# Modulation by raw float32 matmuls in pieces, with the mixer's branches and conv taps in another order

## The chip, the cores and the metric

The program runs on one core of one Trainium2 chip. The metric is the device time of one execution in microseconds; lower is better. The kernel before takes 2353.6 us (median of three runs, 2352.47 to 2354.03).

## The reference

Two blocks follow each other. The change is in the first alone: two layers of a token mixer and a gated FFN on 256 tokens `x` and, in layer 0, 256 context tokens `ctx`, with a modulation vector in front.

```python
for l in range(DEPTH):                                   # DEPTH = 2, D_MODEL = 1024
    mod  = silu(c) @ w_mod[l] + b_mod[l]                 # [1024] @ [1024, 6144]
    modc = silu(c_ctx) @ w_mod[l] + b_mod[l]
    sh1, sc1, gt1, sh2, sc2, gt2 = split(mod, 6)         # and the same of modc for ctx
    h = rms_norm(xl, g_pre_mix[l]) * (1 + sc1) + sh1
    y, yc = token_mixer(h, hc, ...)                      # conv branch, diff attention, pool branch, gates, w_out
    xl = xl + gt1 * rms_norm(y, g_post_mix[l])
    h = rms_norm(xl, g_pre_ffn[l]) * (1 + sc2) + sh2
    xl = xl + gt2 * rms_norm(swiglu(h, w_ffn_in[l], w_ffn_out[l]), g_post_ffn[l])
# token_mixer: g = sigmoid(h @ w_g + b_gate)
# m = g[0:1024] * y_a + g[1024:2048] * y_b + g[2048:3072] * y_c;  return m @ w_out
```

`y_a` is a depthwise convolution of 31 taps with layer norm, `y_b` differential attention of 8 heads, `y_c` a multi-scale pool. All arithmetic is float32. The modulation of a layer reads a weight of 1024 x 6144 and multiplies it by two vectors, `c` and `c_ctx`.

## The kernel before

Activations lie transposed, features on the 128 partitions and tokens in the columns: 512 columns in layer 0 (both streams), 256 in layer 1. A weight of 1 MB (1024 x 256) is loaded by SP into one of two raw buffers, then split into a high part (ACT, L154) and a low part (DVE or POOL, L155) of the float32r type. Each product is three matmuls (`mm3`, L164 to L166). A ring of four split pieces per kind lets `emit` prepare weights ahead of the step that uses them.

The program is a list of steps with costs. `merge` spreads a side list over a main list by cost, and `emit` walks the list. Below it a scheduler sets the order on each engine, and each engine then works through its own queue in that order: what stands in front and waits holds up what is behind.

The modulation of layer 0's first sections (columns 0 to 2047, four groups of 512) is computed in the set-up by `mod` (L433): 32 loads of 128 x 512, each split by L257 and L258, and 64 matmuls of 512 columns (L447, L448) whose stationary side holds the high and low parts of the two vectors in four of 128 columns; `mod_flush` (L498) then copies and transposes the result. The other 20 groups of 512 columns are computed by `mod_v` (L462) on DVE: L476 and L478 multiply 128 x 512 tiles by a scalar per partition and add them up, and a flush (L484) sums over the partitions with matmuls of a 128 x 128 float32 weight tile against one column of ones; L489 adds the bias. Six of these groups run beside the mixer's last branches in layer 0, the rest beside layer 0's FFN. Their loads are 512 KB each in a ring of two (`mraw`).

`mixer1` (L747) orders the mixer of a layer: the gated linear unit of the convolution; then `qkv(0)` with 20 conv taps; four head pairs of attention, each merged with the next pair's q, k, v (the fourth with `gates(0)`) and a quarter of the 104 taps left; then the attention's closing norm `o_fin`, the pool linear with the convolution's layer norm, `w_conv_out` with the pool windows, `gates(2)`, the pool's group products, `w_pool_out`, and at last the gates of the attention and `w_attn_out` in turn. Half of the taps run on DVE (L795), half on ACT and POOL (L792, L793). Scores are half-array matmuls (L742), transposes stand at L869. Between the mixer and FFN0 stands a join: sums over features (L611, L612), the residual and the norm for the second half of the tokens (L316).

Of the kernel before, what the change touches and what calls it, by code (L numbers as in the profile page):

```python
# [26 lines left out]
SHARE = (2, 2, 0, 0, 4, 0, 0, 0)  # of 8 weight pieces, how many GpSimd subtracts, by phase  # L27
SLOTS, RING, MORE, RAWS, US, MRAWS = 66, 4, 4, 2, 6, 2
# [7 lines left out]
class Two:  # L36
    """[128, 8, n] in two tiles"""
# [8 lines left out]
class Kern:  # L46
# [64 lines left out]
    def pieces(self, loads, na, nb, cuts, perm=False):  # L111
        box = {}
        out = []
        for i, (a0, a1, b0, b1) in enumerate(cuts):
# [86 lines left out]
    def lin_pair(self, st, Wa, ca, Wb, cb, n, rhs, N, evac_a, evac_b):  # L201
        """tiles of two column ranges in turn, two by two"""
# [32 lines left out]
    def lin_nat(self, st, W, c0, lhs, ntok, evac):  # L235
        """out [128 tokens, 256 columns]; lhs(t) -> [(hi, lo)] per k tile, [128, 128 tokens]"""
# [50 lines left out]
    def sq_add(self, key, src, N, i, n):  # L287
        """adds src^2 to the running sum self.v[key]"""
# [12 lines left out]
    def col_rms(self, key, nt, dim):  # L301
        """sums over features (partitions) and then 1/rms per token: [128 tokens, nt]"""
# [9 lines left out]
    def bcast(self, r, nt, ps=None, at=0):  # L312
        """[128 tokens, nt] -> PSUM [128, 128 nt]: the same row of tokens on each partition"""
# [29 lines left out]
    def setup(self):  # L343
# [24 lines left out]
        self.st1 = self.const([128, 8, 128], "st1", F32R)  # L368
        nc.vector.memset(self.st1.bitcast(F32), 0.0)
        v = cc.rearrange("p (s k) -> p k s", s=2)  # L370
        nc.vector.tensor_copy(self.st1[:, :, 0:2], v)
        nc.vector.tensor_tensor(self.st1[:, :, 2:4], v, self.st1[:, :, 0:2], op=ALU.subtract)
        self.cc = cc
        self.mc = [self.const([128, 48, 2], f"mc{l}") for l in range(2)]
        nc.gpsimd.memset(self.mc[1], 0.0)
# [57 lines left out]
    def mod(self, l, g):  # L433
        """512 columns on the tensor engine: rows c, c_ctx of the high parts, then of the low parts"""
# [7 lines left out]
        def f():  # L442
            ps = self.lin_ps()
            for k in range(8):
                hi, lo = self.slot(F32R), self.slot(F32R)
                self.split(hi, lo, raw[k])
                nc.tensor.matmul(ps, self.st1[:, k], hi, start=k == 0, stop=False)  # L447
                nc.tensor.matmul(ps, self.st1[:, k], lo, start=False, stop=k == 7)  # L448
            self.mod_flush(l, g, ps)
        return f  # L450

    def pin(self, inst):
        """keeps an instruction that waits for nothing from taking its tile far ahead of its turn"""
        self.tc.keep_in_program_order(inst)

    def mraw(self, l, g, h):
        w = self.wp.tile([128, 2, 512], F32, name=self.nm("mraw"), tag="mraw", bufs=MRAWS)
        self.nc.sync.dma_start(w, self.a["w_mod"][l, 256 * h:256 * h + 256, 512 * g:512 * g + 512].rearrange(
            "(k p) c -> p k c", p=128))
        return w  # L460

    def mod_v(self, st, l, groups, streams):  # L462
        """the same with the products and their sums over k tiles on the vector engine"""
        nc = self.nc
        accs = {}

        def part(g, h):
            w = self.mraw(l, g, h)
            if h == 0:
                accs[g] = [self.slot() for _ in range(streams)]  # L470
            for k in range(2):
                for i in range(streams):
                    acc = accs[g][i]
                    c = self.cc[:, 8 * i + 2 * h + k:8 * i + 2 * h + k + 1]
                    if h == 0 and k == 0:
                        nc.vector.tensor_scalar(acc, w[:, k], c, None, op0=ALU.mult)  # L476
                    else:
                        nc.vector.scalar_tensor_tensor(acc, w[:, k], c, acc, op0=ALU.mult, op1=ALU.add)  # L478

        def flush(g):  # L480
            ps = self.tr_ps()
            for i in range(streams):
                for t in range(4):
                    nc.tensor.matmul(ps[:, 4 * i + t:4 * i + t + 1], accs[g][i][:, 128 * t:128 * t + 128],  # L484
# [1440 lines left out]
```

## Time and profile before

| what | value |
|---|---|
| median of three runs | 2353.6 us (2352.47 to 2354.03) |
| span of the profiled execution, its own time | 2355.8 us |
| PE busy | 2197.7 us, 93% |
| DVE busy | 1707.7 us, 72% |
| ACT busy | 1095.3 us, 46% |
| POOL busy | 536.5 us, 23% |
| matmul records | 14576 |

The span is the time from the first to the last recorded instruction of one profiled execution; the record gives no other time for that execution, so the sums of the prediction stand on 2355.8. PE means the matmuls of TensorE and PEld its weight loads, which overlap them; DVE is VectorE, ACT ScalarE, POOL GpSimd, SP the engine that issues the loads. PEclk in a window is the TensorE clock that was granted, as a share of full speed. The durations of single matmuls overlap, so a cost per matmul is read from the distance between them: a window's length divided by its count.

### The profile page before, as it was taken

The numbers are of one execution on the slowest core, as the hardware profiler recorded it, in microseconds if no ns is written. First come the engines' busy times: TensorE is split into PE (matmuls) and PEld (weight loads), VectorE is DVE, ScalarE is ACT, GpSimd is POOL, SyncE is SP. The second block draws the span as 40 slices with busy tenths as digits, with TensorE's granted clock in tenths as the row PEclk, the third lists the DMA queues.
The fourth block names the chain that finished last, engine by engine and source line by source line (L and its number), as shares of the span: only waits on it lengthen the run. The fifth ranks groups of instructions, "written<-read, shape, count | busy, mean of one in ns | idle before, by whom it ended". The sixth has DMA issues, their size and how long they took to land.

```text
span 2355.8 us, 37801 instructions
## 1 busy us (share of the span) xinstructions
PE 2197.7 (93%) x14576; PEld 1998.8 (85%) x14576; DVE 1707.7 (72%) x3443; ACT 1095.3 (46%) x2110; POOL 536.5 (23%) x545
## 2 busy tenths in 40 slices
PE   4978889999989999989999899999889999999998
PEld 3767777788888888878788899999877999988998
DVE  5697987959678745578988877764686766686665
ACT  5436565332332222244566554554446544465543
POOL 2344433321340110143333312100342000210000
PEclk8989999999999999998999999999987999999999
DMA  7312112335414555553322454455541555542553
GB/s 271 93 55 67 54 59 72 123 132 170 152 63 154 168 179 170 170 165 108 108 72 90 148 174 160 154 193 176 160 90 37 176 183 177 177 144 84 185 180 125
DMA packets 296628, 319.21 MB, mean 135 GB/s; under 512 B 20544, under 2 KB 264352, under 8 KB 296448
## 3 DMA queue, kind: packets, MB, share of 16 engines
q1 hardware_dynamic: 293072, 311.27, 41.1%
q0 software_dynamic: 2224, 3.43, 0.6%
q8 instruction: 114, 1.87, 0.3%
q10 hardware_dynamic: 1152, 2.10, 0.3%
q14 instruction: 66, 0.54, 0.1%
HBM read 315.72 MB, written 1.05 MB: 134 GB/s over the span
## 4 chain that ended last, share of the span: by engine, by line
PE 66%; DVE 21%; issue 4%; ACT 3%; DMA 3%; POOL 1%; SPq 0%; ACTq 0%; DVEq 0%; POOLq 0%
PE p L164 19%; PE p L165 19%; PE p L166 19%; DVE wlo L155 3%; DVE t L795 3%; DVE t L478 2%; DVE t L258 2%; PE p L742 1%; DVE b L851 1%; DMA mraw<-in_w_mod_dram 1%; DVE t L725 1%; PE tr L484 1%; DMA raw<-in_w_in_dram 1%; PE p L247 1%; ACT whi L154 1%
## 5 line engine op out<-in xcount | busy, mean ns | idle before, releaser
L164 PE MATMUL p<-t,whi 128*128 128x256 f32 (+1 forms) x3724 | 1175.5, 320 | 20.8 <-ACT t L560 8.5
L165 PE MATMUL p<-t,whi 128*128 128x256 f32 (+1 forms) x3724 | 1183.0, 319 | 5.6 <-DVE t L561 2.1
L166 PE MATMUL p<-t,wlo 128*128 128x256 f32 (+1 forms) x3724 | 1178.2, 318 | 6.4 <-DVE wlo L155 4.8
L164 PEld LDWEIGHTS p<-t,whi 128*128 128x128 f32 x3724 | 718.8, 195 | 72.6 <-ACT t L560 10.3
L165 PEld LDWEIGHTS p<-t,whi 128*128 128x128 f32 x3724 | 723.6, 194 | 50.8 <-DVE t L659 3.5
L166 PEld LDWEIGHTS p<-t,wlo 128*128 128x128 f32 x3724 | 723.1, 194 | 50.4 <-DVE wlo L155 5.9
L154 ACT ACTIVATE whi<-raw 128x1024 fp32r<-128x1024 f32 (+4 forms) x487 | 492.0, 1020 | 543.4 <-PE p L165 332.6
L155 DVE TENSOR_TENSOR wlo<-raw,whi 128x1024 fp32r<-128x1024 f32 (+4 forms) x443 | 545.4, 1232 | 201.7 <-ACT whi L154 113.7
L155 POOL TENSOR_TENSOR wlo<-raw,whi 128x1024 fp32r<-128x1024 f32 (+2 forms) x44 | 103.5, 2353 | 503.6 <-ACT whi L154 464.8
L478 DVE SCALAR_TENSOR_TENSOR t<-mraw,big,t 128x512 f32<-128x512 f32 x224 | 176.6, 827 | 17.7 <-DMA mraw<-in_w_mod_dram 16.2
L793 POOL TENSOR_TENSOR t<-t,t 128x512 f32<-128x512 f32 (+1 forms) x120 | 134.9, 1125 | 186.0 <-ACT t L792 178.5
L594 POOL TENSOR_TENSOR t<-t,t 128x256 f32<-128x256 f32 (+1 forms) x68 | 70.4, 1063 | 246.1 <-ACT t L596 242.8
L299 POOL TENSOR_TENSOR t<-t,t 128x256 f32<-128x256 f32 (+1 forms) x27 | 25.6, 948 | 430.6 <-ACT t L297 430.1
L260 ACT ACTIVATE t<-t 128x256 fp32r<-128x256 f32 (+1 forms) x115 | 54.3, 473 | 148.9 <-DVE t L689 104.4
L742 PE MATMUL p<-t,t 64*128 64x256 f32 (+2 forms) x528 | 78.5, 374 | 28.5 <-DVE t L261 9.8
L247 PE MATMUL p<-whi,t 128*128 128x256 f32 x352 | 101.8, 289 | 2.8 <-ACT t L853 1.6
L248 PE MATMUL p<-wlo,t 128*128 128x256 f32 x352 | 99.8, 284 | 0.0
L249 PE MATMUL p<-whi,t 128*128 128x256 f32 x352 | 99.8, 283 | 0.0
L689 DVE TENSOR_TENSOR t<-t,p 128x256 f32<-128x256 f32 (+1 forms) x91 | 43.1, 474 | 76.8 <-PE p L166 76.6
L795 DVE SCALAR_TENSOR_TENSOR t<-u,big,t 128x512 f32<-128x512 f32 (+1 forms) x120 | 94.9, 791 | 1.5
L742 PEld LDWEIGHTS p<-t,t 64*128 64x128 f32 x528 | 50.9, 206 | 49.2 <-issue 16.8
L257 ACT ACTIVATE t<-t 128x256 fp32r<-128x256 f32 (+1 forms) x92 | 43.2, 495 | 100.0 <-DVE t L725 80.6
(299 smaller groups left out, 2717.0 us busy)
## 6 DMA issues: line engine op xcount, KB each, us to landing
raw<-in_w_in_dram SPq DMA_DIRECT2D x60, 1024.0 KB, 5.1
raw<-in_l_w_gate_up_dram SPq DMA_DIRECT2D x44, 1024.0 KB, 5.1
raw<-in_w_ffn_in_dram SPq DMA_DIRECT2D x42, 1024.0 KB, 5.3
mraw<-in_w_mod_dram SPq DMA_DIRECT2D x80, 512.0 KB, 4.0
raw<-in_l_w_in_dram SPq DMA_DIRECT2D x15, 1024.0 KB, 5.2
raw<-in_l_w_down_dram SPq DMA_DIRECT2D x16, 896.0 KB, 4.9
t<-in_w_mod_dram SPq DMA_DIRECT2D x32, 256.0 KB, 5.4
raw<-in_w_attn_out_dram SPq DMA_DIRECT2D x8, 1024.0 KB, 5.2
```

Source lines behind the costliest of these rows:

```text
L154: nc.scalar.activation(p.hi, src, AF.Copy)
L155: eng.tensor_tensor(p.lo, src, p.hi, op=ALU.subtract)
L164: mm(ps, lh, rh, start=first, stop=False)
L165: mm(ps, lh, rl, start=False, stop=False)
L166: mm(ps, ll, rh, start=False, stop=last)
L247: mm(ps[:, :256], lh, p.hi[:, k % 4], start=k == 0, stop=False)
L248: mm(ps[:, :256], lh, p.lo[:, k % 4], start=False, stop=False)
L249: mm(ps[:, :256], ll, p.hi[:, k % 4], start=False, stop=k == 7)
L478: nc.vector.scalar_tensor_tensor(acc, w[:, k], c, acc, op0=ALU.mult, op1=ALU.add)
L742: self.nc.tensor.matmul(out[half], q[i // 2][h, qs], k[i % 2][h, ks], start=i == 0, stop=i == 2)
L793: nc.gpsimd.tensor_tensor(acc, acc, t, op=ALU.add)
L795: nc.vector.scalar_tensor_tensor(acc, u, w, acc, op0=ALU.mult, op1=ALU.add)
```

## The change

All of the modulation becomes matmuls with a raw float32 tile of `w_mod` (128 x 128) as the stationary side and the two vectors as two moving columns, summed over eight k tiles in PSUM; one DVE add of the bias ends it. In the set-up the four groups keep their loads, and 128 such products (`mod_mm`, L432 of the changed kernel) take the place of the splits and of the 64 matmuls of 512 columns. The other 80 output tiles become units (`mods`): a 512 KB load into a ring of two, eight products, one add. Forty go among the attention steps of layer 0 (ten per head pair), eight (layer 1's section 0) behind the join in front of FFN0, 32 among the attention steps of layer 1 (10, 10, 10, 2). `mod_v` is gone.

The branches are in another order: `gates(2)` instead of `gates(0)` beside the fourth pair; then the pool branch with `w_pool_out`, which now starts the merged sum; then the rest of `gates(0)`, the convolution's layer norm and `w_conv_out`; the attention's part comes last as before. The 124 taps are spread over a longer stretch: 17 beside `qkv(0)` and each of three pairs, 23 beside the fourth, 33 beside the pool branch.

```diff
-SLOTS, RING, MORE, RAWS, US, MRAWS = 66, 4, 4, 2, 6, 2
+SLOTS, RING, MORE, RAWS, US, MODS = 64, 4, 4, 2, 7, 2
...
+    def mod_mm(self, ps, w, k):
+        c = self.cc.rearrange("p (s k) -> p k s", s=2)[:, k]
+        self.nc.tensor.matmul(ps, w, c, start=k == 0, stop=k == 7)
+    def mod_out(self, l, j, n, ps):
+        b = self.par["b_mod", l][:, j:j + n]
+        self.nc.vector.tensor_tensor(self.mc[l][:, j:j + n, :], ps.rearrange("p (t s) -> p t s", s=2),
+                                     b[:, :, None].to_broadcast([128, n, 2]), op=ALU.add)
...
+            if last:
+                ps = [self.lin_ps()[:, :2] for _ in range(4)]
+                for k in range(8):
+                    for t in range(4):
+                        self.mod_mm(ps[t], raw[k][:, 128 * t:128 * t + 128], k)
...
             ps = self.lin_ps()
-            for k in range(8):
-                hi, lo = self.slot(F32R), self.slot(F32R)
-                self.split(hi, lo, raw[k])
-                nc.tensor.matmul(ps, self.st1[:, k], hi, start=k == 0, stop=False)
-                nc.tensor.matmul(ps, self.st1[:, k], lo, start=False, stop=k == 7)
-            self.mod_flush(l, g, ps)
+            for t in range(4):
+                for k in range(8):
+                    self.mod_mm(ps[:, 2 * t:2 * t + 2], raw[k][:, 128 * t:128 * t + 128], k)
+            self.mod_out(l, 4 * g, 4, ps[:, :8])
...
+        def unit(j):
+            p = Piece()
+            p.ring = 2
+            def prep():
+                p.hi = self.static("mraw", 1024, MODS).rearrange("p (a b) -> p a b", a=8)
+                nc.sync.dma_start(p.hi, self.a["w_mod"][l, :, 128 * j:128 * j + 128].rearrange(
+                    "(k p) c -> p k c", p=128))
+            def f():
+                ps = self.lin_ps()[:, :2]
+                for k in range(8):
+                    self.mod_mm(ps, p.hi[:, k], k)
+                self.mod_out(l, j, 1, ps)
+            p.prep = prep
+            return ("x", 0.9, f, (p,))
+        return [unit(8 * s_ + i) for s_ in secs for i in range(8)]
...
-        out += merge(qkv(0), conv[:20])
-        ncv = len(conv) - 20
+        taps = iter(conv)
+        take = lambda n: [t for _, t in zip(range(n), taps)]
+        out += merge(qkv(0), take(17))
+        fill = iter(fill)
         for pr in range(4):
-            main = qkv(pr + 1) if pr < 3 else gates(0)
-            side = att(pr)
-            out += merge(merge(main, side), conv[20 + pr * ncv // 4: 20 + (pr + 1) * ncv // 4])
-        out.append(X(o_fin))
+            main = qkv(pr + 1) if pr < 3 else gates(2)
+            side = merge(att(pr), [t for _, t in zip(range(10), fill)])
+            out += merge(merge(main, side), take(17 if pr < 3 else 23))
         pl = []
         self.lin(pl, W, 4096, 512, hx, N, pool_evac)
+        out += merge(pl, take(11) + [X(o_fin)])
...
+        g0 = gates(0)
+        out += merge(merge(g0[:4], rest), take(11))
+        gr = groups()
+        b3 = []
+        self.lin(b3, a["w_pool_out"][l], 0, 1024, lambda: V["z"], N, merge_c, K=4)
+        out += gr + merge(b3, list(taps))
         side = [X(conv_ln), X(conv_ln2)] + [X(lambda m=m: conv_ln3(m)) for m in range(4)]
-        out += merge(pl, side)
+        out += merge(g0[4:], side, 1)
...
-            fs = [self.mod(0, g) for g in (2, 3, 0, 1)]
+            fs = [self.mod(0, g, g == 1) for g in (2, 3, 0, 1)]
...
+            fill = self.mods(0, (2, 4, 3, 5)) + self.mods(1, (1,)) if l == 0 else self.mods(1, (2, 4, 3, 5))
...
             st += jm(256 if l == 0 else 0, True)
+            if l == 0:
+                st += self.mods(1, (0,))
...
-                self.mod_v(ms, 0, (10, 11), 2)
...
-                self.mod_v(ms, 1, (2, 3, 0, 1), 2)
-                self.mod_v(ms, 1, (4, 5, 8, 9, 6, 7, 10, 11), 1)
```

How the change stands in the queues is shown at three places on PE. A name such as `p_1315` is a PSUM tile, the buffers behind the arrow are the stationary and the moving side, and a closing `x8` is a row repeated.

In the attention of layer 0, before, the scores (L742) of a head pair follow each other and the next linear tile comes behind them:

```order
L742 MATMUL p_1336<-t_1065,t_970 128x512
L742 MATMUL p_1337<-t_1065,t_970 128x512
L742 MATMUL p_1364<-t_1065,t_969 128x256
L742 MATMUL p_1364<-t_1066,t_969 128x256
L742 MATMUL p_1364<-t_1065,t_970 128x256
L742 MATMUL p_1365<-t_1065,t_969 128x256
L742 MATMUL p_1365<-t_1066,t_969 128x256
L742 MATMUL p_1365<-t_1065,t_970 128x256
L164 MATMUL p_1387<-t_505,whi_1134 128x512
L165 MATMUL p_1387<-t_506,whi_1134 128x512
L166 MATMUL p_1387<-t_505,wlo_1135 128x512
L164 MATMUL p_1387<-t_507,whi_1134 128x512
```

After, units of eight products (L432) stand among the scores (now L722), here two of them in front of the next linear tile:

```order
L722 MATMUL p_1205<-t_969,t_875 128x512
L722 MATMUL p_1206<-t_969,t_875 128x512
L432 MATMUL p_1224<-big,mraw 128x2 x8
L722 MATMUL p_1237<-t_969,t_874 128x512
L722 MATMUL p_1238<-t_969,t_874 128x512
L722 MATMUL p_1237<-t_970,t_874 128x512
L722 MATMUL p_1238<-t_970,t_874 128x512
L722 MATMUL p_1237<-t_969,t_875 128x512
L722 MATMUL p_1238<-t_969,t_875 128x512
L432 MATMUL p_1256<-big,mraw 128x2 x8
L722 MATMUL p_1275<-t_969,t_874 128x256
L722 MATMUL p_1275<-t_970,t_874 128x256
```

So each unit is a block of eight products between pieces of the attention on the same queue.

At the join before FFN0, before, the sums over features (L611, L612) alternate with matmuls of FFN0 for the tokens of the first half (the tile `p_6372`, with `whi_5965` of its weight):

```order
L164 MATMUL p_6372<-t_5899,whi_5965 128x256
L165 MATMUL p_6372<-t_5900,whi_5965 128x256
L166 MATMUL p_6372<-t_5899,wlo_5966 128x256
L164 MATMUL p_6372<-t_5901,whi_5965 128x256
L612 MATMUL tr_6152<-big,t_6142 128x1
L611 MATMUL tr_6152<-big,t_5518 128x1
L612 MATMUL tr_6152<-big,t_6142 128x1
L611 MATMUL tr_6152<-big,t_5520 128x1
L612 MATMUL tr_6152<-big,t_6144 128x1
L611 MATMUL tr_6152<-big,t_5520 128x1
L612 MATMUL tr_6152<-big,t_6144 128x1
L611 MATMUL tr_6152<-big,t_5522 128x1
```

After, units stand between the norm's transposes (L318), and the tile `p_6481` of FFN0 comes behind all eight:

```order
L432 MATMUL p_6376<-big,mraw 128x2 x8
L318 MATMUL tr_6267<-big,c_6251 128x128 x2
L432 MATMUL p_6387<-big,mraw 128x2 x8
L432 MATMUL p_6398<-big,mraw 128x2 x8
L318 MATMUL tr_6267<-big,c_6281 128x128 x2
L432 MATMUL p_6461<-big,mraw 128x2 x8
L432 MATMUL p_6471<-big,mraw 128x2 x8
L166 MATMUL p_6481<-t_6014,whi_6410 128x256
L167 MATMUL p_6481<-t_6015,whi_6410 128x256
L168 MATMUL p_6481<-t_6014,wlo_6411 128x256
L166 MATMUL p_6481<-t_6016,whi_6410 128x256
```

The matmuls of FFN0 that filled the join before are now behind the units, whose loads come through a ring of two buffers.

In the set-up, before, a group's sixteen matmuls of 512 columns (`st` holds the vectors) stand together and the transposes of `x` (L1104) behind them:

```order
L447 MATMUL p_181<-t_218,st_97 128x512
L448 MATMUL p_181<-t_219,st_97 128x512
L447 MATMUL p_181<-t_224,st_97 128x512
L448 MATMUL p_181<-t_225,st_97 128x512
L1104 MATMUL p_273<-big,t_74 128x128
L1104 MATMUL p_273<-big,t_78 128x128
L1104 MATMUL p_273<-big,t_82 128x128
L1104 MATMUL p_273<-big,t_86 128x128
```

After, the first products against two columns lie between those transposes (now L1085):

```order
L432 MATMUL p_176<-big,t_112 128x2
L1085 MATMUL p_244<-big,t_74 128x128
L1085 MATMUL p_244<-big,t_78 128x128
L1085 MATMUL p_244<-big,t_82 128x128
L432 MATMUL p_176<-big,t_114 128x2
L1085 MATMUL p_244<-big,t_86 128x128
L1085 MATMUL p_251<-big,t_74 128x128
L1085 MATMUL p_251<-big,t_78 128x128
L1085 MATMUL p_251<-big,t_82 128x128
L432 MATMUL p_176<-big,t_116 128x2
L1085 MATMUL p_251<-big,t_86 128x128
```

The stationary side is now the loaded tile itself, with no split in front of it.

## Rows read from the trace of the kernel before

**Rows 1.** The page: span, busy time by engine, engines of the last chain

```profile
span 2355.8 us, 37801 instructions
...
PE 2197.7 (93%) x14576; PEld 1998.8 (85%) x14576; DVE 1707.7 (72%) x3443; ACT 1095.3 (46%) x2110; POOL 536.5 (23%) x545
...
PE 66%; DVE 21%; issue 4%; ACT 3%; DMA 3%; POOL 1%; SPq 0%; ACTq 0%; DVEq 0%; POOLq 0%
```

**Rows 2.** Windows of four stages: us, busy us (count) of five engines, PEclk, DMA share

```profile
120.00:160.00 40.00, 28.66 (x176) 24.99 (x174) 39.61 (x53) 13.76 (x24) 17.24 (x13) 0.88 0.24 79
160.00:336.00 176.00, 154.82 (x936) 129.86 (x937) 152.10 (x324) 104.76 (x261) 74.98 (x54) 0.96 0.16 51
336.00:390.00 54.00, 53.20 (x283) 42.60 (x281) 32.61 (x68) 33.82 (x79) 19.57 (x13) 1.00 0.21 70
1157.60:1281.10 123.50, 114.28 (x772) 101.18 (x771) 109.21 (x234) 73.26 (x172) 39.80 (x50) 0.97 0.25 81
```

**Rows 3.** Waits of PE in 160 to 336: us in total, times, longest

```profile
PE p L742 <- DVE t L261: 9.8, 2, 7.0
PE tr L869 <- DVE t L861: 9.3, 9, 1.8
```

**Rows 4.** PE groups by form in 160 to 336: count, busy us, mean ns, idle before

```profile
L164 PE MATMUL p<-t,whi 128*128 128x512 f32 x97 | 41.0, 422 | 2.3 <-DVE t L261 2.3
...
L742 PE MATMUL p<-t,t 64*128 64x256 f32 x69 | 8.6, 316 | 9.8 <-DVE t L261 9.8
```

**Rows 5.** Windows of two flushes and of two dense stretches

```profile
482.94:484.64 1.70, 1.70 (x17) 1.70 (x16) 0.00 (x0) 1.65 (x2) 0.54 (x1) 1.00 1.00 346
1058.88:1061.44 2.56, 2.56 (x13) 2.56 (x14) 0.00 (x0) 0.00 (x0) 0.00 (x0) 0.50 0.00 0
930.00:950.00 20.00, 20.00 (x89) 16.53 (x89) 12.62 (x17) 4.74 (x7) 2.50 (x1) 1.00 0.59 188
1900.00:1950.00 50.00, 50.00 (x419) 50.00 (x418) 33.22 (x53) 24.59 (x36) 0.00 (x0) 1.00 0.57 188
```

**Rows 6.** DVE groups by form: one tap, one add of the modulation

```profile
L795 DVE SCALAR_TENSOR_TENSOR t<-u,big,t 128x512 f32<-128x512 f32 x60 | 60.2, 1003 | 0.7
...
L489 DVE TENSOR_TENSOR big<-tr,big 128x4 f32<-128x4 f32 x32 | 4.3, 156 | 33.5 <-PE tr L484 33.2
```

**Rows 7.** DMA issues: count, KB each, median us to landing

```profile
raw<-in_w_ffn_in_dram SPq DMA_DIRECT2D x4, 512.0 KB, 4.0
```

**Rows 8.** Windows of three neighbouring stretches around 682.7

```profile
679.30:682.70 3.40, 3.40 (x32) 3.40 (x30) 0.00 (x0) 0.54 (x2) 1.66 (x2) 0.97 0.37 127
682.70:686.10 3.40, 3.40 (x18) 3.40 (x18) 2.84 (x22) 0.00 (x0) 0.00 (x0) 0.53 0.00 0
686.10:689.50 3.40, 3.40 (x31) 3.40 (x31) 2.38 (x10) 0.00 (x0) 0.85 (x1) 1.00 0.02 5
```

**Rows 9.** Timeline of PE at the join: start, us, [idle before <-releaser]

```profile
690.58 0.71 PE L316 MATMUL tr<-big,c 128*128 128x128 f32 x4 [0.59 <-DVE c L279]
...
696.70 0.36 PE L164 MATMUL p<-t,t 128*128 128x256 f32 x1 [1.93 <-DVE t L558]
```

**Rows 10.** Source view of L484: its matmuls, what PE sat idle for

```profile
L484 PE MATMUL tr<-big,t x256: 164/250/271, 482.9 to 1080.4; 128*128 128x1 f32 x128
...
  DVE t L478: 3.6, 4
```

**Rows 11.** Timeline of PE in the set-up

```profile
19.68 0.80 PE L447 MATMUL p<-t,st 128*128 128x512 f32 x1 [4.20 <-ACT t L257]
...
28.09 3.65 PE L1104 MATMUL p<-big,t 128*128 128x128 f32 x32
...
62.43 1.20 PE L164 MATMUL p<-t,whi 128*128 128x512 f32 x4 [2.71 <-ACT t L560]
```

**Rows 12.** Timeline of PE: a small matmul before a large one

```profile
82.55 0.27 PE L322 MATMUL tr<-big,t 121*128 121x121 f32 x1
82.58 0.48 PE L164 MATMUL p<-t,whi 128*128 128x512 f32 x1
```

More of the change, by code (lines that the diff above doesn't have):

```diff
@@ L121, in prep @@
                     raw = self.static("raw", 2048, RAWS)
+                    box["n"] = self.rings["raw"][1]
                     box["raw"] = raw[:, : na * nb].rearrange("p (a b) -> p a b", a=na)
@@ L124, in prep @@
                         nc.sync.dma_start(view(box["raw"]), src)
+                assert self.rings["raw"][1] - box["n"] < RAWS
                 src = box["raw"][:, a0:a1, b0:b1]
@@ L430, in setup_rest, with mod @@
             self.par[name] = cols[:, 8 * i:8 * i + 8]
-    def mod(self, l, g):
+    def mod_mm(self, ps, w, k):
[5 more added lines that the diff above has]
+                                     b[:, :, None].to_broadcast([128, n, 2]), op=ALU.add)
+    def mod(self, l, g, last=False):
         nc = self.nc
@@ L454, in pin @@
         self.tc.keep_in_program_order(inst)
[L456 to L462, printed above, removed]
-        nc = self.nc
[L465 to L484, printed above, removed]
-                                     self.ones[:, 0:1], start=True, stop=True)
-            del accs[g]
-            b = self.par["b_mod", l][:, 4 * g:4 * g + 4]
-            for i in range(streams):
-                nc.vector.tensor_tensor(self.mc[l][:, 4 * g:4 * g + 4, i], ps[:, 4 * i:4 * i + 4], b, op=ALU.add)
-        for j, g in enumerate(groups):
-            for h in range(4):
-                st.append(("x", 0.2, lambda g=g, h=h: part(g, h)))
-                if h == 2 and j:
-                    st.append(("x", 0.05, lambda g=groups[j - 1]: flush(g)))
-        st.append(("x", 0.05, lambda: flush(groups[-1])))
@@ L498, in mod_flush, with mods @@
[L498 to L511 removed]
+    def mods(self, l, secs):
+        nc = self.nc
+        def unit(j):
[13 more added lines that the diff above has]
+        return [unit(8 * s_ + i) for s_ in secs for i in range(8)]
@@ L745, in u_tile, with mixer1 @@
         return self.sp.tile([128, 2, 288], F32, name=self.nm("u"), tag="u", bufs=US)
-    def mixer1(self, l, hs, N, evac_y, mid):
+    def mixer1(self, l, hs, N, evac_y, mid, fill=()):
         nc, a = self.nc, self.a
@@ L1067, in mixer1 @@
             self.lin(b2, a["w_attn_out"][l], c, 256, lambda: V["of"], N, lambda m, ps, c=c: merge_b(c // 128 + m, ps))
-        out += merge(b2[:2], [X(lambda h=h: o_tr(h)) for h in range(8)]) + (merge(b2[2:], ms[8:]) if l == 0 else b2[2:])
+        out += merge(b2[:2], [X(lambda h=h: o_tr(h)) for h in range(8)]) + b2[2:]
         wo = []
@@ L1154, in block1 @@
             jm = lambda t0, hot, l=l, N=N: join(l, N, t0, 4, 3, "g_pre_ffn", hot)
-            mix = self.mixer1(l, lambda: self.h, N, y_evac, jm(0, False) if l == 0 else None)
+            fill = self.mods(0, (2, 4, 3, 5)) + self.mods(1, (1,)) if l == 0 else self.mods(1, (2, 4, 3, 5))
+            mix = self.mixer1(l, lambda: self.h, N, y_evac, jm(0, False) if l == 0 else None, fill)
             at = next(i for i in range(len(mix)) if mix[i][0] == "begin")
@@ L1819, in emit @@
 def emit(steps, bufs):
-    order, rings = [], ([], [])
+    order, rings = [], ([], [], [])
     for i, s in enumerate(steps):
```

56 lines of the change are left out of this document (15 added, 41 removed).

## Prediction

> **What bounds the kernel now.** I read the page first: TensorE is busy 93% of the span, and the chain that ended last is 66% PE and 21% DVE [rows 1]. So a matmul added in a dense stretch is paid in full, and only idle time of PE can swallow one. I then cut the stages that the change touches into windows [rows 2]: the three first head pairs of layer 0's attention last 176.0 us with PE busy 154.82 and DVE 152.10; the fourth pair lasts 54.0 with PE busy 53.20; the three first pairs of layer 1 last 123.5, PE 114.28, DVE 109.21. In the attention neither engine is full: PE waits for the split of the keys (9.8 us in two waits) and for the softmax (9.3 in nine) [rows 3]. The work that PE has to do there is less than its busy time. By form (ten rows, of which [rows 4] shows the first and the last), a pair of layer 0 holds 97 matmuls of 512 columns, 144 of 256, 24 transposes (0.114 each) and 47 half-array scores that run two at a time. At the spacings of dense stretches, 20.0 us / 89 = 0.225 and 50.0 / 419 = 0.12 [rows 5], that is 21.8 + 17.3 + 2.7 + 4.1 = 45.9 us, against 176.0 / 3 = 58.7 now. By the same count a pair of layer 1 holds 36.6 of its 123.5 / 3 = 41.2. DVE's own work is 152.10 / 3 = 50.7 and 109.21 / 3 = 36.4.
>
> **The price of a unit.** A unit is 8 matmuls of a float32 tile against two columns, which the profile will write as 16 records. The nearest thing in the trace is the flush at L484: float32 weight tile, one column, two records for a product. Its 16 records took 1.70 us, 0.106 apart, at a granted clock of 1.00 (2.4 GHz), and 12 such records took 2.56 us, 0.213 apart, at 0.50 (1.2 GHz) [rows 5]. Spacing follows the weight load and not the column, so I take a unit at 1.70 us at the full clock, 3.4 at half.
>
> **1. 72 units in the two attentions.** Layer 0 gets 10 units in each pair, 10 x 1.70 = 17.0 us. DVE loses 4.5 taps of 1.003 us in a pair and gains ten small adds of 0.156 [rows 6], so it falls to about 47.8 and PE is the later one: 45.9 + 17.0 = 62.9, and I leave 3 for waits that no unit fills. Three pairs: 3 x (65.9 - 58.7) = +21.6. The fourth pair has 0.8 idle: +16. Layer 1: 3 x (36.6 + 17.0 + 1.5 - 41.2) = +41.7; the two last units +1. Together **+80**. If the units fill every gap it is +66 (12.6 + 16 + 37.2), if they fill none 72 x 1.70 = +122. Each unit's DMA waits on SP until the unit two before it is done, and raw weight loads stand behind it; the same shape of 512 KB lands in 4.0 us [rows 7] while units stand five or six us apart, and prepared weights are four tiles ahead, so I add nothing; where that cover fails it is inside +122.
>
> **2. The clock behind units.** At 682.7 PE runs on without a gap, and the granted clock still goes to 0.53 behind a burst of one-column matmuls: 18 matmuls in 3.4 us where the stretch before had 32 [rows 8]. So a fall costs 14/32 x 3.4 = 1.5 us. At 482.94 a burst of 16 records ran through at 1.00. The units lie between these cases: denser work around them than at 682, more gaps than at 482. I take one in four of 72: 18 x 1.5 = **+27** (0 to 72 x 1.5 = 108).
>
> **3. The join before FFN0.** Before, PE did first halves of FFN0 there and idled 0.59 and 1.93 [rows 9]. Now eight units stand in front of FFN0's matmuls on PE's in-order queue, with two buffers. Two tiles are there early, 3.4 us; then three times a landing of 4.0 [rows 7] and 1.7 to 3.4 of matmuls: 20.5 to 25.6, of which I take 22.5, less the 2.5 of idle that goes: **+20**. If the loads hide, 8 x 1.70 - 2.5 = +11; at worst 25.6 and a fall of 1.5, +27. The SP queue holds the eight loads in a row, and FFN0's own weights stand behind; four of those are loaded ahead.
>
> **4. The flushes go.** 256 records at L484 [rows 10], 16 bursts of 1.70 us: **-27**, all in dense FFN0 and mixer stretches.
>
> **5. DVE's products go** (L478). PE waited for them 3.6 us in four waits [rows 10], and I count one fall of the clock behind these: **-5** (to -10, if DVE's relief also shortens waits for split weights).
>
> **6. The set-up.** Now PE starts the modulation at 19.68 and begins the first layer at 62.43 [rows 11]; it is paced by loads and by the splits on ACT and DVE. After the change the splits are gone, and 128 products of two records stand in their place. With gaps between them and little else to do I expect the half clock: 256 x 0.213 = 54.6 us. With the transposes of x among them, at half the clock twice their 3.65, 7: 19.7 + 54.6 + 7 = 81, and the first matmul of the layer 3 us later, 84: **+22**. At the full clock it would be 19.7 + 27.2 + 3.7 = 50.6, and with the chain to the first layer 52 to 54, which is -9; the loads are through by then.
>
> **7. Branch order and taps.** The first stage of layer 0, where DVE is 39.61 of 40 us busy [rows 2], loses 3 of its 20 tap steps, half of them on DVE: 1.5 x 1.003 = **-1.5**. Where they go DVE has lost its modulation, so I charge them nothing there. The rest of the new order (pool before convolution, two gate rings) issues the same matmuls: 0, from -6 (waits at o_fin and the layer norm hidden) to +8 (pool windows on POOL late for the group matmuls).
>
> Sum: 80 + 27 + 20 - 27 - 5 + 22 - 1.5 = +115.5 on the profiled 2355.8, which is 2471.3. The profiled execution stands 2.2 above the median of 2353.6, so the time that I forecast is **2469 us**.
>
> The Trainium skill bears on term 2 and 6. Its page "TensorE: Matmul & The Clock Gate", section "Why this matters for your kernels", advises to leave no idle gaps between matmul bursts, since idle of PE is what brings the slower clock. By that, units that fill gaps would raise the mean clock of the attention, 0.96 now, and not lower it. The trace differs: at 682.7 the clock fell with PE busy throughout [rows 8]. What the rule would give is the first rival below.
>
> **The rivals.**
> (A) The clock stays full under the units and in the set-up, because PE is never idle there. For it: the burst at 482.94 ran at 1.00, and the attention's clock is 0.96 with its gaps. Against it: the fall at 682.7, and the one-column records at 1058.88 at 0.50. Terms 2 and 6 become 0 and -9, and the join a little shorter, 16: 80 + 16 - 27 - 5 - 9 - 1.5 = +53.5, 2407 us.
> (B) The clock falls behind more than half of the units, 40 x 1.5 = 60, and some of them run at 0.213 themselves, 20 x 1.7 / 2 = 17, with the rest as in the forecast: +115.5 + 33 + 17 = +165, 2519 us. For it: units recur every five or six us. Against it: the dense stretch around 482.94.
> (C) Faster: a two-column record costs no weight load, since the load runs beside the matmul before it. A small matmul in front of a large one did cost just 0.03 us, at 82.55 to 82.58 [rows 12]. If every record of a unit cost 0.03, a unit would be 0.5 us, the 72 units would go into PE's idle (36 us over six pairs), the set-up would end with its loads: 0 + 8 x 0.5 + 9 (loads) - 27 - 5 - 20 - 1.5 = -40, 2313 us. Break-even lies at about 0.07 us per record: 1536 records (1280 in units, 256 in the set-up), less 256 that go. Against it: sixteen records in a row stood 0.106 apart in the dense stretch, so that only the first of a row finds cover.
> (D) It comes out even: gaps take more than I count and the clock stays up in the set-up: +66 becomes +30, 0, +11, -27, -10, -9, -1.5 = -6, some 2348 us or a little above. Nothing speaks for the 30 where the fourth pair of layer 0 alone has 16.
>
> **How the numbers follow.** Forecast 0.59 (2430 to 2500 by itself), A 0.17, B 0.17, C 0.05, D 0.02. The range is 2405 to 2530: it takes in A's and B's times, where the unknown prices of terms 2 and 6 end (less 27 and less 31; plus some 80), and leaves C, D and the far side of B out. Less than 0.2%, 4.7 us, cannot be told from no change here. Faster 0.06, same 0.02, slower 0.92.
>
> **What the changed profile would show.** Records of two columns 0.106 apart in the attention at clock 1.00; a first layer that begins near 84 with a set-up clock near 0.5 (rival A: near 53 at 1.0); pairs of layer 0 of some 66 to 70 us and of layer 1 of some 55 to 60; clock dips of about 3.4 us right behind units, some 18 of them; eight units at the join with PE waiting for loads of 4 us; no L478 or L484. PE records should come to about 14,576 + 1,280 + 256 - 256 - 64 = 15,792. I am wrong if the units' spacing is not 0.1, if the pairs last as long as before, or if the set-up ends before 60.

## The result and the profile after

The changed kernel takes 2516.5 us in the median (2515.5 to 2522.5, four runs) against 2353.0 for the kernel before: a ratio of 1.0696, interval 1.068 to 1.0713. I forecast 2469, slower with a chance of 0.92, and a range of 2405 to 2530. The direction and the range held; the loss is 163.5 us where I had summed 115.5, and the time lies beyond the 2430 to 2500 that I gave the forecast by itself. The profiled execution of after has a span of 2513.7 us, 157.9 above the span before, and the terms below are compared on the spans.

The page of the changed kernel, the rows that answer to [rows 1]: span, busy time by engine (share, instructions), engines of the chain that ended last.

```profile
span 2513.7 us, 39929 instructions
...
PE 2388.8 (95%) x15792; PEld 2195.1 (87%) x15792; DVE 1522.3 (61%) x3183; ACT 1085.7 (43%) x2074; POOL 536.0 (21%) x544
...
PE 83%; DVE 8%; ACT 3%; issue 2%; POOL 2%; DMA 1%; SPq 0%; ACTq 0%; DVEq 0%; POOLq 0%
```

PE has 15,792 records, as counted ahead. DVE lost 185 us of work and its share of the chain fell from 21% to 8%; PE's grew from 66% to 83%. Work went from an engine with slack to the one that sets the end.

To see where the time went I cut both executions at the same events: first score of layer 0, last value product of its attention, first sum of the join before FFN0, end of the join, first score of layer 1, last value product, first sum of the next join, end. Windows of the kernel before (us; busy us and count of PE, PEld, DVE, ACT, POOL; PEclk; DMA share; GB/s):

```profile
0.00:146.00 146.00, 113.67 (x520) 91.74 (x520) 97.75 (x193) 67.70 (x124) 47.43 (x72) 0.95 0.50 161
146.00:391.00 245.00, 211.69 (x1238) 175.07 (x1238) 198.81 (x409) 142.12 (x347) 98.10 (x73) 0.95 0.17 57
391.00:640.00 249.00, 244.23 (x1195) 203.84 (x1195) 198.84 (x305) 87.14 (x128) 69.55 (x53) 0.99 0.46 145
640.00:691.00 51.00, 45.76 (x331) 44.86 (x330) 33.35 (x117) 16.11 (x37) 21.49 (x23) 0.87 0.13 43
691.00:1152.00 461.00, 443.43 (x2404) 387.47 (x2402) 323.58 (x555) 152.74 (x247) 95.98 (x82) 0.97 0.49 155
1152.00:1310.00 158.00, 147.63 (x1037) 132.15 (x1036) 135.43 (x281) 96.13 (x224) 51.08 (x62) 0.98 0.26 87
1310.00:1455.00 145.00, 137.28 (x1111) 135.27 (x1110) 113.82 (x225) 80.72 (x142) 37.85 (x47) 0.98 0.52 168
1455.00:2355.80 900.80, 854.02 (x6754) 828.39 (x6753) 606.13 (x1362) 452.70 (x864) 114.98 (x136) 0.95 0.47 149
```

The same stretches of the changed kernel:

```profile
0.00:164.00 164.00, 146.86 (x711) 132.01 (x711) 71.72 (x142) 48.98 (x87) 45.97 (x70) 0.88 0.46 144
164.00:473.00 309.00, 299.26 (x1874) 263.09 (x1874) 191.69 (x452) 134.33 (x330) 74.83 (x58) 0.90 0.38 113
473.00:717.00 244.00, 235.49 (x1102) 195.02 (x1101) 144.55 (x195) 97.13 (x145) 92.67 (x68) 0.98 0.29 96
717.00:786.60 69.60, 62.01 (x346) 61.57 (x345) 37.09 (x138) 16.86 (x41) 22.70 (x27) 0.63 0.23 69
786.60:1235.00 448.40, 437.83 (x2357) 382.68 (x2357) 211.05 (x362) 152.23 (x241) 92.44 (x76) 0.97 0.31 100
1235.00:1455.00 220.00, 219.96 (x1552) 203.42 (x1552) 137.46 (x314) 94.69 (x210) 37.76 (x47) 0.91 0.45 135
1455.00:1620.00 165.00, 140.31 (x1105) 135.99 (x1103) 121.93 (x224) 86.55 (x157) 53.87 (x64) 0.94 0.45 148
1620.00:2513.70 893.70, 847.12 (x6756) 821.32 (x6756) 606.82 (x1363) 454.95 (x865) 115.74 (x136) 0.96 0.47 150
```

Read the first numbers of each row in pairs:

| stretch | before | after | difference |
|---|---|---|---|
| to the first score | 146.0 | 164.0 | +18.0 |
| attention of layer 0 | 245.0 | 309.0 | +64.0 |
| rest of its mixer | 249.0 | 244.0 | -5.0 |
| join and FFN0, to layer 1's scores | 512.0 | 518.0 | +6.0 |
| attention of layer 1 | 158.0 | 220.0 | +62.0 |
| rest of its mixer | 145.0 | 165.0 | +20.0 |
| to the end | 900.8 | 893.7 | -7.1 |

In layer 1's attention PE is busy 219.96 of 220.00 us, so nothing is waited for there, and yet the granted clock is 0.91 where it was 0.98. At the join it is 0.63 where it was 0.87. The timeline of PE at the join of the changed kernel (start, us, line, count, idle before) shows the units and the clock they run at:

```profile
750.32 4.88 PE L432 MATMUL p<-big,mraw 128*128 128x2 f32 x32
...
756.63 3.55 PE L432 MATMUL p<-big,mraw 128*128 128x2 f32 x16
...
764.74 3.55 PE L432 MATMUL p<-big,mraw 128*128 128x2 f32 x16
769.48 1.19 PE L318 MATMUL tr<-big,c 128*128 128x128 f32 x4 [1.19 <-DVE c L281]
770.46 6.83 PE L432 MATMUL p<-big,mraw 128*128 128x2 f32 x32
778.98 1.22 PE L318 MATMUL tr<-big,c 128*128 128x128 f32 x4 [1.69 <-DVE c L281]
780.00 6.83 PE L432 MATMUL p<-big,mraw 128*128 128x2 f32 x32
786.68 0.56 PE L166 MATMUL p<-t,whi 128*128 128x256 f32 x1
```

From 756.63 on sixteen records take 3.4 us, the half clock of [rows 5], and none of the rows is released by a DMA: the loads were there. In the attention a unit that begins at the full clock takes 1.7 us from its start to the next row, and the set-up runs at the half clock almost throughout, the first layer starting at 77.30 against 62.43 in [rows 11]:

```profile
23.65 11.09 PE L432 MATMUL p<-big,t 128*128 128x2 f32 x52
...
73.68 3.77 PE L432 MATMUL p<-big,t 128*128 128x2 f32 x17
77.30 2.05 PE L166 MATMUL p<-t,whi 128*128 128x512 f32 x4
...
190.43 1.85 PE L432 MATMUL p<-big,mraw 128*128 128x2 f32 x16
192.14 1.19 PE L862 MATMUL tr<-t,t 128*128 128x256 f32 x8
```

The first clock record of this execution is at 39.07. The 0.88 of the set-up's window counts what lies before as full clock, although the 52 records from 23.65 on stand 0.213 us apart; from 42 to 77 the granted clock is 0.51.

### The profile page after: what moved, and what is told of

The parts are those of the page before. It is cut to its first block, busy times and chain, and to the rows that moved or that the text cites. A ratio compares the mean times of both kernels' runs of the same rounds, so it can differ in the third digit from the quotient of the medians.

```text
span 2513.7 us, 39929 instructions
## 1 busy us (share of the span) xinstructions
PE 2388.8 (95%) x15792; PEld 2195.1 (87%) x15792; DVE 1522.3 (61%) x3183; ACT 1085.7 (43%) x2074; POOL 536.0 (21%) x544
## 4 chain that ended last, share of the span: by engine, by line
PE 83%; DVE 8%; ACT 3%; issue 2%; POOL 2%; DMA 1%; SPq 0%; ACTq 0%; DVEq 0%; POOLq 0%
PE p L166 21%; PE p L167 20%; PE p L168 20%; PE p L432 8%; PE p L722 2%; DVE wlo L157 2%; PE tr L862 2%; PE p L249 2%; PE p L251 1%; PE p L250 1%; ACT whi L156 1%; PE tr L849 1%; DVE t L775 1%; PE tr L1249 1%; DMA raw<-in_w_in_dram 1%
## 5 line engine op out<-in xcount | busy, mean ns | idle before, releaser
L166 PE MATMUL p<-t,whi 128*128 128x256 f32 (+1 forms) x3724 | 1182.2, 321 | 20.9 <-ACT t L259 6.5
L432 PEld LDWEIGHTS p<-big,mraw 128*128 128x128 f32 x1280 | 171.3, 214 | 16.4 <-issue 11.8
L432 PE MATMUL p<-big,mraw 128*128 128x2 f32 x1280 | 171.3, 265 | 6.9 <-issue 6.4
L249 PE MATMUL p<-whi,t 128*128 128x256 f32 x352 | 106.6, 303 | 0.0
L251 PE MATMUL p<-whi,t 128*128 128x256 f32 x352 | 104.0, 295 | 0.0
L437 DVE TENSOR_TENSOR big<-p,big 128x2 f32<-128x2 f32 (+1 forms) x87 | 13.6, 156 | 138.8 <-PE p L432 138.8
L722 PE MATMUL p<-t,t 64*128 64x256 f32 (+2 forms) x528 | 81.9, 389 | 14.9 <-DVE t L698 7.5
L262 ACT ACTIVATE t<-t 128x256 fp32r<-128x256 f32 (+1 forms) x115 | 54.2, 472 | 89.3 <-DVE t L669 71.0
L775 DVE SCALAR_TENSOR_TENSOR t<-u,big,t 128x512 f32<-128x512 f32 (+1 forms) x120 | 88.9, 741 | 1.7
## 6 DMA issues: line engine op xcount, KB each, us to landing
mraw<-in_w_mod_dram SPq DMA_DIRECT2D x80, 512.0 KB, 3.8
```

The source lines that it names most:

```text
L166: mm(ps, lh, rh, start=first, stop=False)
L249: mm(ps[:, :256], lh, p.hi[:, k % 4], start=k == 0, stop=False)
L251: mm(ps[:, :256], ll, p.hi[:, k % 4], start=False, stop=k == 7)
L432: self.nc.tensor.matmul(ps, w, c, start=k == 0, stop=k == 7)
L722: self.nc.tensor.matmul(out[half], q[i // 2][h, qs], k[i % 2][h, ks], start=i == 0, stop=i == 2)
L775: nc.vector.scalar_tensor_tensor(acc, u, w, acc, op0=ALU.mult, op1=ALU.add)
```

## The experiments

My theory: the price is PE time, first of the records themselves (0.106 us each), and then of the half clock that the two-column products bring. Rivals: the queues and the two load buffers hold PE up; the clock falls because of waits and not because of the columns; the new branch order and not the modulation loses the time. Seven kernels were run; the ratio is always to the kernel before on the same chip.

**e1: 128 moving columns.** The two vectors are repeated 64 times by a broadcast on the moving side; the sum uses two columns of the result. Shown are the lines that widen; those that pick the two columns out again are left out.

```diff
-        c = self.cc.rearrange("p (s k) -> p k s", s=2)[:, k]
-        self.nc.tensor.matmul(ps, w, c, start=k == 0, stop=k == 7)
+        c = self.cc.rearrange("p (s k) -> p k s", s=2)[:, k:k + 1].to_broadcast([128, 64, 2])
+        self.nc.tensor.matmul(ps.rearrange("p (r s) -> p r s", s=2), w, c, start=k == 0, stop=k == 7)
```

> The changed kernel with one thing altered: the moving side of each product against w_mod repeats the two vectors 64 times (128 columns instead of 2; the sum uses the first two). Theory 1 (the few columns bring the half clock): a product of 128 columns still takes two records 0.106 to 0.114 apart, the clock stays at 1.00 under the units and in the set-up, the first layer begins near 52 instead of 77.3, the half clock in the two attentions falls from 64.9 and 41.0 us towards the 23.9 and 6.8 of before, and the time falls by 45 to 75, to 2440 to 2470. Rival (the falls come from gaps and waits of the in-order queue, not from the columns): the clock is as after, the time 2506 to 2526. Second rival (the columns are paid): records stand over 0.2 apart at full clock, 1536 x 0.1 more, over 2600.

Measured: 2455.9 us (2448.9 to 2457.9), ratio 1.042 (1.0383 to 1.0456), some 60 us less than the changed kernel. Windows of the set-up and of the two attentions, cut at the same events:

```profile
0.00:138.00 138.00, 119.82 (x710) 106.52 (x710) 70.97 (x142) 48.82 (x87) 45.75 (x70) 1.00 0.54 171
138.00:436.00 298.00, 278.51 (x1865) 243.35 (x1864) 193.39 (x452) 134.23 (x329) 75.86 (x58) 0.98 0.39 115
...
1189.00:1390.00 201.00, 201.00 (x1543) 186.65 (x1540) 137.94 (x312) 93.33 (x208) 40.15 (x47) 1.00 0.49 147
```

and two rows of its timeline:

```profile
47.80 7.33 PE L435 MATMUL p<-big,t 128*128 128x128 f32 x64
54.88 0.48 PE L169 MATMUL p<-t,whi 128*128 128x512 f32 x1
```

64 records stand (54.88 - 47.80) / 64 = 0.111 us apart. The clock is 1.00 in the set-up (from 23.06 on, where its records begin) and in layer 1's attention, with PE as full as in the changed kernel, 201.00 of 201.00. Only the width of the moving side differs, so in layer 1 the two-column products brought the half clock, not waits. The first layer begins at 54.88. Theory 1 holds against both rivals.

**e2: the modulation of after, the branch order and taps of before.** The first places of the edit; behind the attention the order goes back likewise, and so do the numbers of buffers (`SLOTS` 66, `US` 6).

```diff
-        out += merge(qkv(0), take(17))
+        out += merge(qkv(0), conv[:20])
...
-            main = qkv(pr + 1) if pr < 3 else gates(2)
+            main = qkv(pr + 1) if pr < 3 else gates(0)
             side = merge(att(pr), [t for _, t in zip(range(10), fill)])
-            out += merge(merge(main, side), take(17 if pr < 3 else 23))
+            out += merge(merge(main, side), conv[20 + pr * ncv // 4: 20 + (pr + 1) * ncv // 4])
```

> The changed kernel's modulation with the branch order and the taps of before (20 beside qkv(0), 26 a pair, gates(0) beside the fourth pair). Theory 1 (the new order costs in layer 1, where a 9.2 us wait of PE on the memory norm stands, and in layer 0 some 5): the stretch from the end of layer 1's attention to the next join, 165 us after, goes back towards 145, and the time is 2488 to 2503. Rival (the new order relieves the attention of taps, and that is worth as much): the pairs grow by as much as the rest shrinks, 2511 to 2525.

Measured: 2495.3 us (2493.7 to 2505.2), ratio 1.0602 (1.0568 to 1.0635). Windows: attention and rest of the mixer of layer 0, and the rest of layer 1's:

```profile
164.00:478.00 314.00, 303.87 (x1870) 267.75 (x1871) 191.53 (x453) 145.15 (x347) 95.94 (x73) 0.88 0.37 111
478.00:717.00 239.00, 233.50 (x1106) 194.46 (x1105) 136.23 (x194) 86.59 (x128) 71.14 (x53) 0.99 0.30 99
...
1451.00:1598.00 147.00, 138.62 (x1106) 136.73 (x1104) 113.87 (x224) 79.31 (x141) 37.40 (x47) 0.97 0.51 166
```

The time is in the range of theory 1. The new order costs 18 us in layer 1 (165 against 147). In layer 0 it gives 5 in the attention (309 against 314) and loses 5 behind it (244 against 239). The 5 that it gives are not sure: with the steps of the changed kernel there, this attention takes 313.3 us in e5 and 311.7 in e6. So in layer 0 the new order is even at best.

**e3: one of eight products in each unit.** Loads, adds and order stay; the sums of the modulation are incomplete.

```diff
-                for k in range(8):
-                    self.mod_mm(ps, p.hi[:, k], k)
+                c = self.cc.rearrange("p (s k) -> p k s", s=2)[:, 0]
+                nc.tensor.matmul(ps, p.hi[:, 0], c, start=True, stop=True)
```

> The changed kernel with seven of the eight products of each of the 80 units left out (loads, adds and the order stay; the sums of the modulation are incomplete). Theory 1 (the units' records on PE and the half clock behind them are the price): 1120 records at 0.12 go, 134 us, idle of some 35 comes back, and some 25 of half clock goes: 2380 to 2410. Rival (the loads through two buffers and the order on the queues hold PE up, not the records): 2460 to 2516.

Measured: 2379.8 us, one run, just below theory 1's 2380 to 2410. The two attentions:

```profile
163.00:413.00 250.00, 225.58 (x1311) 188.89 (x1311) 192.23 (x452) 133.48 (x330) 74.56 (x55) 0.92 0.47 139
...
1158.00:1315.00 157.00, 153.16 (x1099) 138.09 (x1099) 135.53 (x313) 91.71 (x208) 40.78 (x47) 0.99 0.63 187
```

With all loads and adds but few records the attentions take 250 and 157 us, as long as before the change (245 and 158). The 72 loads that stand there, through two buffers, cost nothing that could be seen; the records do.

**e4: the kernel before with only the set-up as raw products of 128 columns.** The edit for three of the four groups; the last has its loops the other way round, as in the changed kernel.

```diff
-            for k in range(8):
-                hi, lo = self.slot(F32R), self.slot(F32R)
-                self.split(hi, lo, raw[k])
-                nc.tensor.matmul(ps, self.st1[:, k], hi, start=k == 0, stop=False)
-                nc.tensor.matmul(ps, self.st1[:, k], lo, start=False, stop=k == 7)
-            self.mod_flush(l, g, ps)
+            for t in range(4):
+                for k in range(8):
+                    self.mod_mm(ps[:, 128 * t:128 * t + 128], raw[k][:, 128 * t:128 * t + 128], k)
+            self.mod_out(l, 4 * g, 4, ps.rearrange("p (t c) -> p t c", t=4)[:, :, :2])
```

> The kernel before with the set-up's modulation alone done by raw float32 products, with the vectors repeated to 128 columns; all else as before. Theory 1 (at the full clock the 256 records need 28 us, less than the splits and loads take now): the first layer begins at 50 to 56 instead of 62.4, and the time falls by 6 to 12, to 2341 to 2347. Rival (the loads or the chain through the adds and h set the start, or the half clock stays): first layer at 60 or later, 2350 to 2365.

Measured: 2350.6 us (2346.5 to 2358.1, ten runs) against 2357.9 on that chip (13 runs), ratio 0.9977 (0.9961 to 0.9993). Its timeline of PE:

```profile
32.50 21.62 PE L434 MATMUL p<-big,t 128*128 128x128 f32 x192
53.88 0.48 PE L167 MATMUL p<-t,whi 128*128 128x512 f32 x1
```

The first layer begins at 53.88 instead of 62.43, 8.6 us earlier; the span ends 6.6 us earlier (2349.2). The medians on this chip lie 7.3 us apart, where theory 1 had 6 to 12; its 2341 to 2347 were counted from the 2353 of another chip. This version is 0.2% faster than the kernel before: the interval leaves out 1, but the gain is small.

**e5: the memory norm of layer 1 in another place.** In the changed kernel PE's transposes of the memory norm wait 9.2 us, the longest wait behind layer 1's attention:

```profile
PE tr L1298 <- DVE t L1292: 9.2, 1, 9.2
```

```diff
-        if l == 1:
-            rest.append(X(lambda: self.mem_norm(0)))
...
-        out += b1
+        out += merge(b1, [X(lambda: self.mem_norm(0))]) if l == 1 else b1
```

> The changed kernel with one step of layer 1 moved: the memory norm stands beside w_conv_out and no longer beside the pool windows and the first half of gates(0). Theory 1 (in the new order PE's transposes of the memory norm wait 9.2 us behind DVE's pool windows and taps, and the clock stays half for some 17 us after it): the stretch from the end of layer 1's attention to the join, 165 us after and 145 before, falls to 148 to 155, and the time is 2499 to 2508. Rival (PE waits as long for the pool windows themselves, the norm is only the first to wait): the wait goes to another line, 2512 to 2521.

Measured: 2508.1 us (2503.7 to 2509.7), ratio 1.0656 (1.0632 to 1.068). The waits of PE and the window of that stretch:

```profile
PE p L166 <- ACT t L1014: 4.5, 1, 4.5
...
PE tr L1296 <- DVE t L1290: 2.8, 1, 2.8
```

```profile
1451.60:1604.60 153.00, 138.88 (x1111) 136.39 (x1111) 122.59 (x225) 87.72 (x160) 54.75 (x64) 0.97 0.49 161
```

The stretch falls from 165 to 153. Theory 1 had 148 to 155. One step's place in the queue is worth 12 of the 18 us, and a wait of 4.5 on ACT takes part of its room. The median falls by 8 only, from a kernel measured on another chip, and the intervals of the two ratios touch at 1.068: the gain is read from the stretch and not from the whole time.

**e6: the join's eight units spread over FFN0.**

```diff
-            if l == 0:
-                st += self.mods(1, (0,))
...
-                fs = merge(fs, [X(lambda: begin(0, 5, "g_post_ffn"))])
+                fs = merge(merge(fs, [X(lambda: begin(0, 5, "g_post_ffn"))]), self.mods(1, (0,)))
```

> The changed kernel with the eight units at the join spread over FFN0's steps. Theory 1 (at the join the units ran at half clock and pushed 13.7 us of FFN0's matmuls behind them): the join, 69.6 us with the units, goes back to some 51 and its half clock from 51.0 to some 14 us, the units cost 8 x 1.7 = 14 in FFN0, and the time is 2494 to 2504. Rival (eight units cost PE the same wherever they stand): 2511 to 2521.

Measured: 2512.0 us (2509.3 to 2515.3), ratio 1.0672 (1.0645 to 1.0698): the rival's time. Windows of the join, of the stretch to layer 1's scores, and of the rest of layer 1's mixer:

```profile
722.90:777.40 54.50, 49.90 (x352) 48.95 (x352) 33.94 (x120) 16.12 (x37) 21.31 (x23) 0.84 0.16 49
777.40:1227.90 450.50, 436.13 (x2357) 380.15 (x2357) 212.44 (x380) 152.52 (x245) 93.71 (x80) 0.98 0.33 104
...
1446.80:1618.50 171.70, 145.39 (x1111) 141.31 (x1109) 122.90 (x225) 87.20 (x159) 54.22 (x64) 0.89 0.44 143
```

Locally theory 1 holds: the join is 54.5 at a clock of 0.84, and join and FFN0 together take 505.0 us instead of 518.0. But the first scores come 3.2 us later, layer 0's attention takes 2.7 more, and the rest of layer 1's mixer 6.7 more at a clock of 0.89 (0.94 in after). That last stretch also took 171.0 us in e1 and 172.0 in e3, at clocks of 0.92 and 0.89, and all three leave its steps as they are in the changed kernel. So its clock differs between executions, 165 to 172 us is the new order's spread there (147.0 and 148.1 with the old order, in e2 and e7), and the 6.7 says nothing of this edit. The ratio cannot be told from that of the changed kernel; the 13 us at the join are read from the windows.

**e7: 128 columns, the old order, and the join's units in FFN0 together.** Its diff is that of e1, e2 and e6.

> The units with all that the runs before pointed to: 128 moving columns, the branch order and taps of before, the join's units in FFN0. Theory 1 (what is left is the records' own time on PE): 2353, less 9 for the set-up, plus 53 and 43 for the attentions as with 128 columns, plus 15 for the units in FFN0, less 33 for flushes and DVE's products: 2422, between 2412 and 2432. Rival (the losses overlap, and with 26 taps a pair the attention is longer again): 2435 to 2450.

Measured: 2441.0 us (2437.8 to 2442.3), ratio 1.0372 (1.035 to 1.0394): the rival's time. Its two attentions:

```profile
138.20:443.70 305.50, 284.60 (x1867) 246.35 (x1866) 197.75 (x453) 143.98 (x346) 94.37 (x73) 0.96 0.38 113
...
1192.90:1394.40 201.50, 201.46 (x1545) 186.94 (x1544) 139.82 (x313) 99.19 (x223) 49.85 (x62) 1.00 0.49 147
```

Layer 0's attention takes 305.5 us instead of e1's 298.0, which is 7.5 of the 19 us between the sum and the result. PE idles there 20.9 us against 19.5 in e1, and the half clock lasts 23.9 us against 13.7, by the clock records of the traces: most of the 7.5 is clock, and that the 26 taps a pair bring it is not shown. The rest of layer 0's mixer, the join and FFN0 give back 12 us together, where the sum had 33 - 15 = 18. What remains over before lies in the attentions, 60.5 + 43.5 us; the records' own time there is 72 x 1.81 = 130 us, of which a part fell into idle.

## Why the prediction was right, and where its sizes were off

The direction was right for the reason given: the products cost PE time, and they cost clock (e1, e3). That the measured 2516.5 stands beside rival B's 2519 is chance. B wanted 40 falls of the clock and 20 units at the half clock. The clock records show 12 new falls in the attentions, and of the 72 units there 62 ran at the full clock throughout, 3 at the half and 7 across a change. About half of what my sum lacked, 20 of 42 us, lies in the branch order, which no rival had. So the range held partly by luck: its upper end stood on B.

**Units in the attentions: +80 predicted, about +91 measured.** In e1, where the clock is nearly full, the attentions are 53 and 43 us longer than before. A unit takes 1.81 us there from its start to the next matmul, and 1.74 in the changed kernel where the clock is full (medians over the trace), so two columns alone cost 72 x 0.07 = 5 less: 91. Layer 0 holds about 50 of it, where I had 38, layer 1 about 41, of 43. Units filled less of layer 0's idle than I allowed; the price of one, 1.70, was about right. From the first score of one pair to that of the next, the first three pairs take 83.9, 71.2 and 74.5 us in layer 0, where I had 66 to 70, and 62 in layer 1, where I had 55 to 60.

**The clock behind units: +27 predicted, about +35 measured.** It is what the attentions lost, 126, less the 91. The split is not sharp: e1 has 13.7 us of half clock in the attentions and the kernel before 30.7, so the records may take up to 8 us more, and the clock so much less. The mechanism is the one of [rows 8]: the clock fell with PE busy. I forecast 18 falls; the clock records show 17 stretches at half clock in the two attentions, but 5 were there before, so 12 came in. What was mis-sized is the length of one: I took 3.4 us from [rows 8], and the 17 last 106 us together, 6.2 each; the 12 new ones add 75 us, which at half speed is at most 38 us of work. Windows around one of them in the changed kernel:

```profile
247.50:250.90 3.40, 3.40 (x27) 2.84 (x28) 3.20 (x7) 1.90 (x4) 0.73 (x1) 0.97 0.85 293
250.90:254.30 3.40, 3.30 (x17) 2.69 (x13) 2.57 (x7) 3.22 (x9) 1.27 (x1) 0.50 0.54 159
254.30:257.70 3.40, 3.40 (x15) 2.87 (x15) 1.89 (x9) 0.00 (x0) 0.00 (x0) 0.50 0.35 104
257.70:261.10 3.40, 3.40 (x13) 2.62 (x11) 0.85 (x3) 0.00 (x0) 0.00 (x0) 0.52 0.17 50
261.10:264.50 3.40, 3.40 (x18) 2.76 (x17) 1.60 (x5) 2.29 (x7) 0.83 (x1) 1.00 0.00 0
```

The clock stays half through three of these windows while PE is busy in all of them.

**The join: +20 predicted, about +26 measured, and by another cause.** I let PE wait for loads of 4 us. It never did; the units ran at the half clock, most of them 3.4 us each, and hold PE for 25.6 us by the rows above. Join and FFN0 together are +6.0: these 25.6, less 17.0 for the flushes (160 of the 256 records), less 4.6 of PE's idle (22.8 before, 18.2 after), plus some 2 for other matmuls. Before, the trace counts 269 of the three-matmul records within the join, and after only 155; the other 114, at 0.12 us some 14 us, now run in FFN0. That moves time from one stretch to the other and is no price of its own. e6 gives 13 us back, about what eight units cost more at the half clock than at the full (25.6 against 14). Of the steps, this is the one whose mechanism failed.

**Flushes and DVE's products: -27 and -5 predicted.** With the old order (e2) the rest of layer 0's mixer is 10 us shorter than in the kernel before, which is the 96 flush records there at 0.106. For FFN0 the two are not measured apart from the join. Term 5 misread its row: the 3.6 us in four waits of [rows 10] count the idle time of PE's weight loads beside that of its matmuls. The waits of PE's matmuls alone (us, times, longest), before:

```profile
PE tr L484 <- DVE t L478: 1.4, 2, 1.0
```

So these waits were worth 1.4 us and not 3.6. The size came out all the same for FFN0, where PE's idle went from 17.6 to 10.6 us, most of it at other lines: this is what the term had in brackets, fewer waits once DVE had less to do.

**Set-up: +22 predicted, +14.9 to the first layer and +18.0 to the first score.** The half clock came as expected. The 84 was too late because the products began at 17.13 and not at 19.7, because some 28 of the 256 records ran at the full clock (39.34 to 42.48, some 3 us), and because the first layer followed the last record without the 3 us that I had added. e1 and e4 show the other end: 53.9 to 54.9 for the first layer, where I had 52 to 54.

**Branch order and taps: 0 predicted within -6 to +8, +20 measured in layer 1's mixer.** I weighed it in layer 0, where by e2 it is even at best, and did not look at the memory norm, which in layer 1 moved to a place behind DVE's pool windows and taps. In the order of after that step stands beside the first half of `gates(0)`; the wait of 9.2 us and the clock that fell behind it were readable as a rival and were not among mine. Of the 42 us between my sum and the span, 25 lie in the new order (20 here and 5 behind layer 0's attention, which may have come back inside it, see e2), 11 in the units, 8 in the clock, 8 at the join and FFN0 (+6.0 where the terms gave 20 - 17 - 5); set-up and first taps give 2.5 back and the last stretch 7.

The Trainium skill's advice to leave no idle gaps between matmul bursts (page "TensorE: Matmul & The Clock Gate", section "Why this matters for your kernels") does not cover this case: in layer 1's attention of the changed kernel PE is busy 219.96 of 220.00 us at a clock of 0.91, and with 128 columns 201.00 of 201.00 at 1.00. The measurement decides: a busy PE was not enough here, and the width of the moving side made the difference.

The last stretch, -7.1 us, was not touched by the change; it is between 891 and 898 in e1, e2, e3, e5, e6 and e7 and 900 in e4. By the clock records it held 82.7 us of half clock before and 64.8 after, and half of that difference, 9.0, is enough for the 7.1. The other runs go the same way: 60 to 65 us where it is 891 to 894, and 79 to 80 where it is 897 to 900. Why the clock fell there less I did not settle.

## What to carry to other kernels

A matrix-vector product is cheap only on an engine with slack: on PE a 128 x 128 float32 weight tile costs two records of some 0.11 us, with 2 columns or with 128, and in attentions where PE was 86 and 93% busy about 91 of the 125 us of 72 units landed in the end time. If such products must stand on PE, try a moving side widened by a broadcast: here that lifted the clock of the matmuls around them, from 0.91 to 1.00 in layer 1's attention. And when steps are reordered, follow every step that shares a queue with the moved ones, in each layer: one norm behind a busy DVE cost more than the whole reordering was thought to.

## What was not expected of the hardware

The broadcast moving side of 128 columns costs hardly more than 2 columns (1.81 us a unit against 1.74, medians at the full clock; within a unit the records of both stand 0.112 us apart in the median). It lifts the granted clock of the changed kernel's set-up from 0.51 (42 to 77) to 1.00 (18 to 55 in e1) and of its attentions from 0.90 and 0.91 to 0.98 and 1.00. The set-up is 26 us shorter by it, the attentions 30 and the join 13; other stretches are 8 longer, and the kernel is some 60 of 2516 faster. And in e3 the attentions' 72 loads of 512 KB with two buffers, issued in front of other loads on the same queue, left them at 250 and 157 us, close to the 245 and 158 without such loads.
